# A trunk of four layers: TensorE's order in the third is written by hand, and its triangular blocks are inverted by doubling

## The chip, the cores and the metric

The kernel runs on one core of a Trainium2 chip. The metric is the device time of one execution in microseconds; for each kernel the median of several runs is given.

## What is computed

A trunk of four layers works on a sequence of 256 context and 1024 grid tokens with 1024 features: an RG-LRU layer, an mLSTM layer, an RWKV-7 layer (layer 2, the only one that the change touches) and an RG-LRU layer again. All in fp32. Cut to layer 2:

```python
def rwkv7_mixer(hc, hx, rows, ...):
    def run(h, shifted, states):
        xs = h[None] + (shifted - h)[None] * mu[:, None, None, :]          # six mixtures
        r, k, v, z = einsum('gbtd,gde->gbte', xs[:4], w_rkvz)
        w_pre = w0 + tanh(xs[4] @ w1) @ w2;  decay = exp(-exp(-softplus(-w_pre) - 0.5))
        a = sigmoid(a0 + (xs[5] @ a1) @ a2)
        kk = hd(k * k_k);  kk = kk / max(sqrt(sum(kk * kk)), 1e-12)
        ...
        yf, sf = rwkv7_scan(r, w[0], kk, a[0], k[0], v, states[0], False)   # forward
        yb, sb = rwkv7_scan(r, w[1], kk, a[1], k[1], v, states[1], True)    # backward
    ...
    return (finish(*parts_c) if with_ctx else None), finish(*parts_x)      # norm, bonus, gate, @ w_out

def rwkv7_scan(...):                                                       # per token
    s = s * w_t - (s @ kk_t) (kk_t * a_t)^T + v_t k_t^T;   y_t = s @ r_t
```

The kernel computes the scan in chunks of 64 tokens: inside a chunk the token recurrence becomes a unit triangular system of 64 x 64 for each head, which is inverted, and matmuls with the inverse carry the state from chunk to chunk.

## The kernel before

All of layer 2 is in `rwkv_scan`. The 1280 tokens are five blocks of 256, block 0 being the context. A batch `n` (0 to 39) is a pair of heads `e` and a place `i` in the order of the blocks: forward the blocks run 0, 1, 2, 3, 4, backward 0, 4, 3, 2, 1, and a batch holds both directions. Four pairs of heads follow each other at each `i`, so that the state of one pair, `st[e % 4]`, is needed again four batches later. Two waves of 20 batches cover the 8 pairs.

For each batch:
- `prep(n)` loads the projected rows, computes decay and gate, makes the operands `BK`, `AR`, `X`, multiplies them (line 1093) and cuts the products into the diagonal 32 x 32 blocks `DG`, the off-diagonal ones `OF`, and `RB`; it also transposes to `BT` (line 1111) and computes the bonus (line 1131).
- `inverse(n)` inverts the eight 64 x 64 triangles (2 directions, 4 chunks) of both heads: VectorE transposes `DG` to `LN` (line 1147, 1024 wide), inverts the 16 x 16 blocks by forward substitution in 14 pairs of small operations (lines 1164 and 1165), transposes back to `DF` (line 1167), and TensorE doubles twice: from 16 to 32 (lines 1177 and 1182, with the mask `DO` by GpSimd, `QQ` copied by ScalarE, `D32` added and `E32` transposed by VectorE) and from 32 to 64 (lines 1189 and 1195). The result is `DT`.
- `chain(n, step)` carries the state over one chunk in each direction: four groups of matmuls with a copy or an addition between them (lines 1236, 1240, 1246, then 1253 and 1255 for the output).
- `finish(n)` normalizes the output rows of a pair and writes them.

Beside the scan stand the projections: `group` (the mixtures made by `mixed`, eight operands of 128 features as a rounded part and a remainder, and then the products with the weights, three matmuls for each product) and `output` (the product with the output weights). `project` and the code for `v` (lines 924 to 926) issue them, `half` loads 512 columns of weights and splits them. `kk_norm` normalizes the keys. The list `fill` says which projections are issued in which iterations, and how many.

In an iteration of the main loop the code asks for four steps of `chain`, `finish(n - 2)`, `inverse(n + 1)`, `prep(n + 2)` and its share of the projections, in this order. This is no order on the engines: the kernel is built with a planner (`schedule_with_timeline_sim=True`) that lays out each engine's queue at compile time by its own estimate of when an instruction could start; `issue_after` only holds projections behind VectorE's work of three iterations ago. Each engine then takes its queue strictly in that order.

PSUM has eight banks: two for the projections (`pz`), two for `prep` and `finish` (`px`), three for the chain (`pc`), one for `inverse` and `kk_norm` (`pi`).

Of the kernel before, what the change touches and what calls it, by code (L numbers as in the profile page):

```python
# [28 lines left out]
class Net:  # L29
# [756 lines left out]
    def rwkv_scan(self, es, hd, zd, yd, xd):  # L786
# [107 lines left out]
        def project(w_ap, xs, n):  # L894
            ps = bank(pz, "pz")[:, 0:n]
            for k in range(len(xs)):
                if k % 4 == 0:
                    w = half(w_ap[:, k * 128:k * 128 + 512])
                self.mm3(ps, w, k % 4, xs[k], (0, n), k == 0, k == len(xs) - 1)
            return ps  # L900

# [3 lines left out]

        def group(blks, what, wave=0):
            n = 256 * len(blks)
            for g in what:
                xs = [mixed(g, k, blks) for k in range(8)]
                if g >= 4:  # L910
                    ps = project(self.a["r7_l1"][g - 4], xs, n)
                    t = tile_("po", [128, 512], bufs=3)
                    S.activation(out=t[:, 0:n], in_=ps, func=AF.Tanh if g == 4 else AF.Copy)
                    out_blocks(blks, lambda b: ld[b][:, g - 4, :], t)
                    yield
                elif g == 2:
                    for i, b in enumerate(blks):
                        for q in (wave,):
                            acc = [bank(pz, "pz") for _ in range(2)]
                            for k in range(8):  # L920
                                w = half(self.a["r7_wv"][q][:, k * 512:k * 512 + 512])
                                for c in range(2):
                                    tk = slice(i * 256 + c * 128, i * 256 + c * 128 + 128)
                                    mm(acc[c], xs[k][0][:, tk], w[0], start=k == 0, stop=False)
                                    mm(acc[c], xs[k][0][:, tk], w[1], start=False, stop=False)
                                    mm(acc[c], xs[k][1][:, tk], w[0], start=False, stop=k == 7)
                                if k == 3:
                                    yield
                            for c in range(2):
                                t = tile_("po", [128, 512], bufs=3)  # L930
                                S.copy(out=t, in_=acc[c])
                                for j in (0, 1):
                                    nc.sync.dma_start(out=vd[b][8 * q:8 * q + 8, :, 2 * c + j, :].rearrange("h s v -> s h v"),
                                                      in_=t[hr[j]].rearrange("p (h v) -> p h v", h=8))
                            yield
                else:
                    for e in range(4 * wave, 4 * wave + 4):
                        ps = project(self.a["r7_w"][g, e], xs, n)
                        t = tile_("po", [128, 512], bufs=3)
                        if g == 3:  # L940
                            S.activation(out=t[:, 0:n], in_=ps, func=AF.Tanh, scale=0.5)
                            self.stt(V, t[:, 0:n], t[:, 0:n], 1.0, ps, ALU.add, ALU.mult)
                            out_blocks(blks, lambda b: zd[e][:, b * 256:(b + 1) * 256], t)
                        else:
                            S.copy(out=t[:, 0:n], in_=ps)
                            out_blocks(blks, lambda b: krk[b][e, :, 1 - g, :], t)
                        if g == 1:
                            kk_norm(e, t, n, blks)
                        yield

        def output(blks, ks, src):

            n = 256 * len(blks)
            xs = []
            for k in ks:
# [8 lines left out]
                xs.append((hi, lo))  # L964
            s = 0 if blks[0] else 1
            for e in range(8):
                t = tile_("po", [128, 512], bufs=3)
                for i, b in enumerate(blks):
                    nc.sync.dma_start(out=t[:, i * 256:(i + 1) * 256], in_=src[e][:, b * 256:(b + 1) * 256])
                ps = project(self.a["r7_w_out"][e][:, ks[0] * 128:], xs, n)  # L970
                self.stt(V, t[:, 0:n], ps, gate[:, e, s:s + 1], t[:, 0:n], ALU.mult, ALU.add)
                out_blocks(blks, lambda b: xd[e][:, b * 256:(b + 1) * 256], t)
                yield

        def kk_norm(e, kt, n, blks):

            sq = tile_("kq", [128, 512], bufs=1)
            S.activation(out=sq[:, 0:n], in_=kt[:, 0:n], func=AF.Square, scale=kk_v[:, e:e + 1])
            nt = n // 128
            ps = bank(pi, "pi")  # L980
# [7 lines left out]
            ps = bank(pi, "pi")  # L988
# [27 lines left out]
        def prep(n):  # L1016
# [13 lines left out]
            DG = DGs[n % len(DGs)]  # L1030
            b["DG"], b["OF"] = DG, tile_("OF", [128, 8, 32])
            ts, ops = [], []
            for d in (0, 1):
# [43 lines left out]
                X = tile_("X%d" % d, [128, 4, 2, 128], bufs=3)  # L1077
                for hh in (0, 1):
                    r = hr[hh]
                    self.tt(G if hh else V, X[r, :, hh, :], AR[r], W[r].unsqueeze(2).to_broadcast([64, 4, 128]))  # L1080
                b[d] = dict(X=X, W=W)
                ts.append((t, rx))
                ops.append((BK, AR))
            for d in (0, 1):
                BK, AR = ops[d]
                X = b[d]["X"]
# [4 lines left out]
                for c in range(4):  # L1091
                    for hh, r in enumerate(hr):
                        mm(pss[hh][:, c * 128:(c + 1) * 128], BK[r, c, 64 - 64 * hh:192 - 64 * hh], AR[r, c, :], start=True, stop=True)  # L1093
                for hh in (0, 1):
# [12 lines left out]
            for d in (0, 1):  # L1107
                for c in range(4):
                    for hh in (0, 1):
                        o = d * 256 + c * 64  # L1110
                        nc.tensor.transpose(tp[hh][:, o:o + 64], ops[d][0][hr[hh], c, 64 - 64 * hh:192 - 64 * hh], self.ident[hr[hh], hr[hh]])
            for hh in (0, 1):
                S.copy(out=BT[:, :, :, hr[hh]], in_=tp[hh].rearrange("p (d c s) -> p d c s", d=2, c=4))
# [4 lines left out]
            else:  # L1118
                ps = bank(px, "px")
                for d in (0, 1) if i else (1,):  # L1120
# [8 lines left out]
                    for q in (0, 1):  # L1129
                        o = 4 * d * (i > 0) + 2 * q  # L1130
                        mm(ps[:, o:o + 2], tp[:, q * 128:(q + 1) * 128], rkb[:, e, :], start=True, stop=True)
                m = 8 if i else 4
# [5 lines left out]
        def inverse(n):  # L1138
# [5 lines left out]
            l8 = lambda name, tag=None: rp.tile([128, 8, 32], F32, tag=tag or name, name=name, bufs=1)  # L1144
# [4 lines left out]
            full = LN.rearrange("p t s -> p (t s)")  # L1149

            def ap(t0, tn, s0, sn, tb, sb):

                v = full[:, t0 * 32 + s0:t0 * 32 + s0 + 1]
                dims = [list(v.ap[0]), [16 * 33, 2], [0 if tb else 32, tn], [0 if sb else 1, sn]]
                return bass.AP(v.tensor, v.offset, dims)

            for j in range(1, 15):
                n1 = 15 - j
                tmp = tile_("ltmp", [128, 2, 56], bufs=1)
                c = ap(j + 1, n1, j, j, False, True)  # L1160
                x = ap(j, n1, 0, j, True, False)
                o = ap(j + 1, n1, 0, j, False, False)
                tv = tmp[:, :, 0:n1 * j].rearrange("p q (t s) -> p q t s", s=j)
# [4 lines left out]
            D16, E16 = l8("D16"), l8("E16", "E")  # L1168
            self.tt(V, D16, DF[:, 0:8, :], u8(m16))
            self.tt(V, D16, D16, u8(id32), ALU.add)  # L1170
            V.transpose(out=E16, in_=D16)
            p8 = lambda: pi.tile([128, 8, 64], F32, tag="pi", name="pi")
            ps = p8()
            g4 = [slice(32 * g, 32 * g + 32) for g in range(4)]
            for u in range(8):
                for g in g4:
                    mm(ps[g, u, 0:32], DO[g, u, :], E16[g, u, :], start=True, stop=True)
            QQ = l8("QQ", "Q8")
            S.copy(out=QQ, in_=ps[:, :, 0:32])
# [332 lines left out]
```

## Time and profile before

| | |
|---|---|
| median of 3 runs | 4717.35 us (4715.73 to 4727.37) |
| profiled execution | 4715.13 us |
| its span | 4713.0 us |
| TensorE busy | 4093.5 us (87%) |
| VectorE busy | 3313.9 us (70%) |
| GpSimd busy | 2271.5 us (48%) |
| ScalarE busy | 2110.1 us (45%) |
| granted clock of TensorE, mean | 0.855 |

Busy times are those of the profiled execution, the shares are of its span. A granted clock of 1.00 is 2.4 GHz, of 0.50 is 1.2 GHz; a value between is the mean over a stretch in which both were granted. Shares over the whole span mix four layers; the scan of layer 2 runs from about 2026 us to 4131 us of the span.

### The profile page before, as it was taken

Reading aid. Unit: us, or ns where it says so; the run is one execution under the profiler, and the core shown is the slowest. Engines: PE = TensorE matmul, PEld = TensorE weight load, DVE = VectorE, ACT = ScalarE, POOL = GpSimd, SP = SyncE. Lnnn points to the kernel's source line nnn. Section 1 sums busy time; section 2 is a strip of 40 time slices with the busy share of each in tenths; the row PEclk is TensorE's granted clock in tenths of the full one; section 3 lists DMA queues with packets and bytes.
Section 4 is the critical chain, followed back from the end, with each engine's and each line's share of the span. In section 5 each row is a group of like instructions: output and inputs, shape, how many; then the busy total and the mean of one; then the engine's idle time right before and its main releaser. Section 6 shows DMA issues by size and latency. Waiting matters only on the chain. (4 is left out here: it accounts for less than half of the span.)

```text
span 4713.0 us, 84318 instructions
## 1 busy us (share of the span) xinstructions
PE 4093.5 (87%) x32068; PEld 3313.0 (70%) x32068; DVE 3313.9 (70%) x6218; ACT 2110.1 (45%) x4476; POOL 2271.5 (48%) x1989
## 2 busy tenths in 40 slices
PE   6999888999999989668988888888898888779988
PEld 3687768988889868445667666666666676557767
DVE  4478656545545533687988888988889889658875
ACT  3576322222222210645656545445566434256661
POOL 2466533333333331366666545555456654356662
PEclk9999989999999999768788777667588787689989
DMA  5311422222222342434444333223244443321122
GB/s 202 116 51 51 141 90 77 90 88 92 88 88 88 116 136 71 157 119 131 139 134 142 121 102 109 88 91 106 85 139 129 148 154 114 100 99 52 47 95 97
DMA packets 317749, 504.50 MB, mean 107 GB/s; under 512 B 55168, under 2 KB 201600, under 8 KB 317216
## 3 DMA queue, kind: packets, MB, share of 16 engines
q1 hardware_dynamic: 317344, 499.12, 33.1%
q8 instruction: 252, 4.13, 0.4%
q14 instruction: 153, 1.25, 0.1%
HBM read 406.02 MB, written 92.96 MB: 106 GB/s over the span
## 5 line engine op out<-in xcount | busy, mean ns | idle before, releaser
L86 POOL TENSOR_TENSOR wlo<-wraw,whi 128x512 fp32r<-128x512 f32 (+3 forms) x437 | 713.8, 1635 | 922.5 <-DVE whi L101 453.3
L112 PE MATMUL pm<-hhi,wlo 128*128 128x512 f32 (+1 forms) x1648 | 611.9, 374 | 32.1 <-POOL wlo L86 32.1
L111 PE MATMUL pm<-hlo,whi 128*128 128x512 f32 (+1 forms) x1648 | 620.1, 377 | 9.9 <-DVE hlo L81 9.9
L110 PE MATMUL pm<-hhi,whi 128*128 128x512 f32 (+1 forms) x1648 | 617.7, 375 | 0.6 <-ACT hhi L288 0.6
L101 DVE CAST whi<-wraw 128x1024 fp32r<-128x1024 f32 (+4 forms) x189 | 170.0, 900 | 336.5 <-PE pm L111 171.1
L86 POOL TENSOR_TENSOR xl<-mx,xh 128x512 fp32r<-128x512 f32 (+1 forms) x240 | 288.6, 1205 | 221.1 <-ACT xh L881 181.7
L110 PE MATMUL pz<-xh,whi 128*128 128x512 f32 (+1 forms) x784 | 333.8, 428 | 51.2 <-ACT whi L890 22.0
L112 PEld LDWEIGHTS pm<-hhi,wlo 128*128 128x128 f32 x1648 | 316.0, 192 | 87.2 <-POOL wlo L86 37.8
L111 PEld LDWEIGHTS pm<-hlo,whi 128*128 128x128 f32 x1648 | 316.0, 192 | 65.8 <-DVE hlo L81 11.4
L110 PEld LDWEIGHTS pm<-hhi,whi 128*128 128x128 f32 x1648 | 316.8, 192 | 53.8 <-issue 1.7
L111 PE MATMUL pz<-xl,whi 128*128 128x512 f32 (+1 forms) x784 | 330.1, 422 | 22.1 <-POOL xl L86 18.2
L110 PE MATMUL pm<-yhi,whi 128*128 128x512 f32 (+1 forms) x816 | 303.9, 377 | 44.5 <-DVE x L81 16.2
L112 PE MATMUL pz<-xh,wlo 128*128 128x512 f32 (+1 forms) x784 | 329.5, 421 | 6.7 <-POOL wlo L86 4.9
L111 PE MATMUL pm<-ylo,whi 128*128 128x512 f32 (+1 forms) x816 | 304.7, 374 | 3.9 <-POOL ylo L86 3.3
L112 PE MATMUL pm<-yhi,wlo 128*128 128x512 f32 (+1 forms) x816 | 297.9, 372 | 1.6 <-POOL wlo L86 1.6
L81 DVE SCALAR_TENSOR_TENSOR x<-pm,mod,x 128x512 f32<-128x512 f32 (+1 forms) x208 | 136.6, 665 | 184.3 <-PE pm L112 168.2
L1093 PE MATMUL px<-AR,BK 64*128 64x128 f32 x1280 | 204.3, 362 | 67.1 <-ACT BK L1071 37.6
L110 PEld LDWEIGHTS pz<-xh,whi 128*128 128x128 f32 x784 | 175.5, 225 | 94.9 <-ACT xh L881 28.2
L1093 PEld LDWEIGHTS px<-AR,BK 64*128 64x128 f32 x1280 | 171.9, 253 | 93.4 <-ACT BK L1071 46.1
L890 ACT CAST whi<-wraw 128x512 fp32r<-128x512 f32 x276 | 169.7, 617 | 142.5 <-PE pz L111 47.6
L81 DVE SCALAR_TENSOR_TENSOR mx<-hp,vecs,mx 128x256 f32<-128x256 f32 (+3 forms) x280 | 198.4, 731 | 46.3 <-ACT mx L861 45.5
L1164 DVE TENSOR_TENSOR ltmp<-LN 128x28 f32<-128x28 f32 (+6 forms) x560 | 219.0, 391 | 12.1
(356 smaller groups left out, 11041.3 us busy)
## 6 DMA issues: line engine op xcount, KB each, us to landing
wraw<-in_r_w SPq DMA_DIRECT2D x144, 256.0 KB, 3.1
kin<-r7krk SPq DMA_DIRECT2D x72, 384.0 KB, 3.3
mw<-in_mod_w SPq DMA_DIRECT2D x48, 512.0 KB, 6.9
mw<-in_mod_w SPq DMA_DIRECT2D x96, 256.0 KB, 2.6
wraw<-in_lru_w_in SPq DMA_DIRECT2D x40, 512.0 KB, 3.6
hp<-r7h SPq DMA_DIRECT2D x160, 128.0 KB, 2.2
wraw<-in_r_wv SPq DMA_DIRECT2D x80, 256.0 KB, 3.1
UZ<-r7v SPq DMA_DIRECT2D x160, 128.0 KB, 2.9
```

Of the source, the lines that this page charges most:

```text
L81: i = eng.scalar_tensor_tensor(out=out, in0=in0, scalar=scalar, in1=in1, op0=op0, op1=op1, **k)
L86: eng.tensor_tensor(out=out, in0=a, in1=b, op=op)
L101: nc.vector.tensor_copy(out=hi, in_=raw)
L110: mm(out, w[0][:, c], x[0][:, a:a + b], start=first, stop=False)
L111: mm(out, w[0][:, c], x[1][:, a:a + b], start=False, stop=False)
L112: mm(out, w[1][:, c], x[0][:, a:a + b], start=False, stop=last)
L890: S.copy(out=hi, in_=raw)
L1093: mm(pss[hh][:, c * 128:(c + 1) * 128], BK[r, c, 64 - 64 * hh:192 - 64 * hh], AR[r, c, :], start=True, stop=True)
L1164: V.tensor_tensor(out=tv, in0=c, in1=x, op=ALU.mult)
```

## The change

`group` and `output` no longer issue their matmuls themselves. They yield passes (`rows` or `cols`), and `stream` issues one step of a pass at a time (three matmuls of up to 512 columns, or six for `v`), asks for weight halves two ahead, makes one operand of the next job behind each step of the pass before it, and puts the two later parts of `kk_norm` into the next pass, where they take a bank of `pz`. Each `yield` says what the step cost, one unit being a pass of 512 columns.

`prep`, `inverse`, `chain` and `finish` become generators with a `yield` between the pieces that wait for each other. In an iteration each piece has a time between 0 and 40 units; the pieces are issued in the order of these times, and between two of them `project` issues projections for `rate` units per unit of time. The amounts per iteration are 132 units (iterations 0 and 1), 84 (2 to 5), 46.5 (6 to 37) and 32 (38 to 40). At the end every TensorE instruction of the scan is tied behind the one before it, so that the planner can't change TensorE's order; the other engines' queues are still the planner's.

`inverse` no longer substitutes on VectorE. It starts from the blocks of size 1 (the identity) and doubles five times, sizes 1, 2, 4, 8 and 16, each time with a mask of `DG` (`lev`) by GpSimd; the first is an addition, the other four are the two groups of 32 matmuls that the last one was before, with ScalarE's copy between them and VectorE's addition and transpose behind. `DG` shrinks from 32 blocks to 8 and has two buffers.

The diff, cut (moved code of `group`, `output` and `prep` is left out where only its place changes):

```diff
+        def rows(job, w_ap, done):
+            n, ks = job.n, len(job.tiles)
+            hs = [w_ap[:, k * 128:k * 128 + 512] for k in range(0, ks, 4)]
+            def steps():
+                ps = bank(pz, "pz")[:, 0:n]
+                for k in range(ks):
+                    yield lambda w: self.mm3(ps, w, k % 4, job.xs[k], (0, n), k == 0, k == ks - 1)
+                done(ps)
+            return job, hs, 4, steps, 3 * n / 512
...
+        def stream(passes):
...
+            for pi_, (job, h, per, steps, cost) in enumerate(passes):
+                nxt = passes[pi_ + 1][0] if pi_ + 1 < len(passes) else job
+                while len(job.xs) < len(job.tiles):
+                    job.make()
+                if not ready:
+                    ahead()
+                for k, step in enumerate(steps()):
+                    if k % per == 0:
+                        if k:
+                            ready.pop(0)
+                        if len(ready) < 2:
+                            ahead()
+                    step(ready[0])
+                    if late and k in (2, 5):
+                        next(late[0], None)
+                        if k == 5:
+                            late.pop()
+                    if nxt is not job:
+                        nxt.make()
+                    yield cost
+                ready.pop(0)
+            drain(*late)
...
         def kk_norm(e, kt, n, blks):
             sq = tile_("kq", [128, 512], bufs=1)
             S.activation(out=sq[:, 0:n], in_=kt[:, 0:n], func=AF.Square, scale=kk_v[:, e:e + 1])
+            yield
             nt = n // 128
-            ps = bank(pi, "pi")
+            ps = bank(pz, "pz")
...
-            DO = l8("DO")
-            LN = tile_("LN", [128, 32, 32], bufs=1)
-            V.transpose(out=LN, in_=DG.rearrange("p u t -> p t u"))
-            self.tt(G, DO, DG[:, 0:8, :], u8(off16))
...
-            for j in range(1, 15):
...
-                V.tensor_tensor(out=tv, in0=c, in1=x, op=ALU.mult)
-                V.tensor_tensor(out=o, in0=tv, in1=o, op=ALU.add)
-            DF = tile_("DF", [128, 32, 32], bufs=1)
-            V.transpose(out=DF.rearrange("p u t -> p t u"), in_=LN)
...
+            O = l8("O")
+            self.tt(G, O, DG, u8(lev[0]))
+            D32, E32 = l8("D"), l8("E")
+            self.tt(V, D32, O, u8(id32), ALU.add)
             V.transpose(out=E32, in_=D32)
+            yield
+            for m in lev[1:]:
+                O = l8("O")
+                self.tt(G, O, DG, u8(m))
+                ps = p8()
+                for u in range(8):
+                    for g in g4:
+                        mm(ps[g, u, 0:32], O[g, u, :], E32[g, u, :], start=True, stop=True)
+                yield
+                QQ = l8("QQ", "Q8")
+                S.copy(out=QQ, in_=ps[:, :, 0:32])
+                for u in range(8):
+                    for g in g4:
+                        mm(ps[g, u, 32:64], QQ[g, u, :], D32[g, u, :], start=True, stop=True)
+                yield
+                D, E32 = l8("D"), l8("E")
+                V.tensor_tensor(out=D, in0=D32, in1=ps[:, :, 32:64], op=ALU.add)
+                V.transpose(out=E32, in_=D)
+                D32 = D
...
+        lev = [cst(f"lev{size}", [128, 32], 0.0) for size in (1, 2, 4, 8, 16)]
...
+            for m, size in zip(lev, (1, 2, 4, 8, 16)):
...
+                sel(v, [[-2 * size, nb], [0, size]], 0, 1)
+                sel(v, [[2 * size, nb], [0, size]], size - 1, -1)
...
+        fill = [(stream(group(G1, (4, 5) + krv)), 0, 2, 336), (stream(group(G2, (4, 5) + krv)), 2, 6, 336),
+                (stream(both(*(group(g, krv, 1) for g in (G0, G1, G2)), *(group(g, (3,), w) for g in (G0, G1, G2) for w in (0, 1)),
+                             output(G0, range(8), self.xsrc), output(G1, range(4), self.xsrc), output(G2, range(4), self.xsrc))), 6, 38, 1488),
+                (stream(output(G2, range(4, 8), xd)), 38, 41, 96)]
+        INV = (10, 12, 14, 16, 18, 20, 22, 24, 26, 28.5, 31, 33, 36)
...
+        for n in range(41):
+            dense, a, z, total = next(f for f in fill if f[1] <= n < f[2])
+            rate = (total - 72 * (a == 0)) / (z - a) / 40
...
+            for c, step, t in ((n - 1, 2, 0), (n - 1, 3, 16), (n, 0, 10), (n, 1, 26)):
+                if 0 <= c < 40:
+                    gens.append(at(chain(c, step), (t, t + 4, t + 8, t + 12, t + 14)))
+            if n < 39:
+                gens.append(at(preps[n + 1], (1, 5, 9, 11, 12)))
+                gens.append(at(inverse(n + 1), INV))
+            if n < 38:
+                preps[n + 2] = at(prep(n + 2), (13, 17, 19))
             if n > 1:
-                finish(n - 2)
+                gens.append(at(finish(n - 2), (3, 21, 23)))
+            t0 = 0
+            for t, _, g in sorted(events, key=lambda v: v[:2]):
+                if t > t0:
+                    project(rate * (t - t0))
+                    t0 = t
+                next(g, None)
+            project(rate * (40 - t0))
...
+        last = None
+        for i in nc.cur_bb.bb.instructions[mark:]:
+            if str(i.engine).split(".")[-1] == "PE":
+                if last is not None:
+                    self.tc.add_manual_dep(i, last.name, mybir.DependencyInfo(mybir.DependencyClass.NoSync, mybir.DependencyReason.DATA), reason="order")
+                last = i
```

## Rows read from the trace of the kernel before

**Rows 1.** Busy us of each engine in two stretches of the scan.

```profile
core 0: us, PE busy (x) PEld busy (x) DVE busy (x) ACT busy (x) POOL busy (x), PEclk, DMA share, GB/s
2026.00:2407.00 381.00, 305.61 (x2597) 217.86 (x2595) 319.50 (x592) 212.44 (x490) 242.42 (x225) 0.78 0.43 131
2407.00:4034.00 1627.00, 1379.56 (x16384) 1083.39 (x16383) 1418.06 (x3052) 844.70 (x2279) 897.73 (x963) 0.75 0.38 117
```

**Rows 2.** One line's instructions, 2407 to 4034: duration ns min/median/max, first, last start.

```profile
L1147 DVE STREAM_TRANSPOSE LN<-DG x34: 1932/1991/2124, 2407.0 to 4033.6; 128x1024 f32<-128x1024 f32 x34
```

**Rows 3.** Groups by line, 2020 to 4050: count | busy us, mean ns | idle before.

```profile
L1164 DVE TENSOR_TENSOR ltmp<-LN 128x28 f32<-128x28 f32 (+6 forms) x560 | 219.0, 391 | 12.1
L1165 DVE TENSOR_TENSOR LN<-ltmp,LN 128x28 f32<-128x28 f32 (+6 forms) x560 | 215.7, 385 | 12.7
...
L1147 DVE STREAM_TRANSPOSE LN<-DG 128x1024 f32<-128x1024 f32 x40 | 80.5, 2013 | 12.2 <-ACT DG L1099 11.5
...
L86 DVE TENSOR_TENSOR D<-DF,m 128x256 f32<-128x256 f32 x39 | 25.3, 650 | 0.5
...
L86 DVE TENSOR_TENSOR D<-D,id 128x256 f32<-128x256 f32 x39 | 21.7, 556 | 0.5
...
L1171 DVE STREAM_TRANSPOSE E<-D 128x256 f32<-128x256 f32 x39 | 16.9, 434 | 4.7 <-PE pi L1189 4.2
L1184 DVE TENSOR_TENSOR D<-D,pi 128x256 f32<-128x256 f32 x39 | 16.1, 414 | 10.7 <-PE pi L1182 10.3
```

**Rows 4.** The same view: one doubling level on the other engines.

```profile
L1177 PE MATMUL pi<-E,DO 32*32 32x32 f32 x2496 | 39.0, 209 | 17.9 <-DVE E L1171 13.1 <-DVE kq L81 4.8
...
L1182 PE MATMUL pi<-D,QQ 32*32 32x32 f32 x2496 | 36.8, 211 | 4.0 <-ACT QQ L1179 3.9
...
L86 POOL TENSOR_TENSOR DO<-DG,off 128x256 f32<-128x256 f32 x40 | 31.8, 795 | 31.6 <-ACT DG L1099 20.4 <-PE pi L1177 9.5 <-DVE ltmp L1164 1.6
...
L1179 ACT COPY QQ<-pi 128x256 f32<-128x256 f32 x39 | 14.5, 372 | 7.0 <-PE pi L1177 6.7
```

**Rows 5.** TensorE in order of time at granted clock 1.00: start us, us.

```profile
2626.97 0.50 PE L925 MATMUL pz<-wlo,xh 128*128 128x512 f32 x1
2627.31 0.39 PE L926 MATMUL pz<-whi,xl 128*128 128x512 f32 x1
2627.54 0.40 PE L925 MATMUL pz<-wlo,xh 128*128 128x512 f32 x1
...
2628.56 0.45 PE L1253 MATMUL pc<-UZ,X 128*64 128x64 f32 x8
...
2629.58 0.75 PE L1177 MATMUL pi<-E,DO 32*32 32x32 f32 x64
```

**Rows 6.** The same view at granted clock 0.50.

```profile
2605.74 1.08 PE L1182 MATMUL pi<-D,QQ 32*32 32x32 f32 x64 [3.91 <-ACT QQ L1179]
2606.75 0.80 PE L925 MATMUL pz<-wlo,xh 128*128 128x512 f32 x1
2607.34 0.63 PE L926 MATMUL pz<-whi,xl 128*128 128x512 f32 x1
2607.77 0.63 PE L925 MATMUL pz<-wlo,xh 128*128 128x512 f32 x1
...
3334.38 0.69 PE L1253 MATMUL pc<-UZ,X 128*64 128x64 f32 x8
```

**Rows 7.** Busy us of each engine in two stretches of one clock each (columns as rows 1).

```profile
2799.00:2829.00 30.00, 26.98 (x429) 21.41 (x419) 20.17 (x49) 15.74 (x42) 14.93 (x18) 1.00 0.39 120
...
3308.00:3427.00 119.00, 101.30 (x1252) 82.93 (x1251) 104.05 (x254) 62.94 (x180) 49.23 (x61) 0.50 0.28 81
```

**Rows 8.** Projections alone (bank pz): PE, PEld, DVE, ACT busy; clock, DMA, GB/s.

```profile
2799.00:2829.00 30.00, 10.18 (x41) 7.47 (x41) 0.00 (x0) 1.17 (x2) 1.00 0.39 120
...
3308.00:3427.00 119.00, 17.88 (x60) 13.54 (x59) 0.77 (x2) 1.93 (x4) 0.50 0.28 81
...
2407.00:4034.00 1627.00, 559.02 (x1939) 376.93 (x1938) 29.92 (x48) 34.33 (x65) 0.75 0.38 117
```

**Rows 9.** One tile's instructions: duration ns min/median/max, first and last start.

```profile
L812 POOL TENSOR_SCALAR_AFFINE_SELECT mk<-mk x8: 231/234/243, 1911.9 to 1914.3; 64x64 f32<-64x64 f32 x8
```

More of the change, by code (lines that the diff above doesn't have):

```diff
@@ L892, in half @@
             return hi, lo
[L894 to L900, printed above, removed]
         def out_blocks(blks, dst, t):
@@ new lines, in cols, with steps, mms @@
+        def cols(job, i, w_ap, done):
+            def steps():
+                acc = [bank(pz, "pz") for _ in range(2)]
+                for k in range(8):
+                    def mms(w):
+                        for c in range(2):
+                            tk = slice(i * 256 + c * 128, i * 256 + c * 128 + 128)
+                            mm(acc[c], job.xs[k][0][:, tk], w[0], start=k == 0, stop=False)
+                            mm(acc[c], job.xs[k][0][:, tk], w[1], start=False, stop=False)
+                            mm(acc[c], job.xs[k][1][:, tk], w[0], start=False, stop=k == 7)
+                    yield mms
+                for c in range(2):
+                    done(c, acc[c])
+            return job, [w_ap[:, k * 512:k * 512 + 512] for k in range(8)], 1, steps, 6
@@ new lines, in stream, with ahead @@
+        def stream(passes):
+            passes = list(passes)
+            hs = [ap for _, h, *_ in passes for ap in h]
+            ready = []
+            nh = 0
+            def ahead():
+                nonlocal nh
+                if nh < len(hs):
+                    ready.append(half(hs[nh]))
+                    nh += 1
+            for pi_, (job, h, per, steps, cost) in enumerate(passes):
[20 more added lines that the diff above has]
+            drain(*late)
@@ L916, in group @@
                 elif g == 2:
                     for i, b in enumerate(blks):
[L918 to L935, printed above, removed]
@@ L1167, in inverse @@
-            V.transpose(out=DF.rearrange("p u t -> p t u"), in_=LN)
[L1168 to L1171, printed above, removed]
+            l8 = lambda name, tag=None: rp.tile([128, 8, 32], F32, tag=tag or name, name=name, bufs=2 if name in "DO" else 1)
             p8 = lambda: pi.tile([128, 8, 64], F32, tag="pi", name="pi")
-            ps = p8()
             g4 = [slice(32 * g, 32 * g + 32) for g in range(4)]
-            for u in range(8):
-                for g in g4:
-                    mm(ps[g, u, 0:32], DO[g, u, :], E16[g, u, :], start=True, stop=True)
@@ L1178, in inverse @@
-            QQ = l8("QQ", "Q8")
-            S.copy(out=QQ, in_=ps[:, :, 0:32])
-            for u in range(8):
-                for g in g4:
-                    mm(ps[g, u, 32:64], QQ[g, u, :], D16[g, u, :], start=True, stop=True)
-            D32, E32 = l8("D32"), l8("E32", "E")
-            V.tensor_tensor(out=D32, in0=D16, in1=ps[:, :, 32:64], op=ALU.add)
-            V.transpose(out=E32, in_=D32)
+            O = l8("O")
+            self.tt(G, O, DG, u8(lev[0]))
+            D32, E32 = l8("D"), l8("E")
@@ L1314, in rwkv_scan @@
             nc.sync.dma_start(out=h0[k // 4][:, k % 4, :], in_=hd[k][:, 0:256])
-        for _ in group((0,), (4, 5, 1, 0, 2)):
-            pass
+        drain(stream(group((0,), (4, 5, 1, 0, 2))))
         early = False
@@ L1346, in rwkv_scan @@
         sgs = [cst(f"sg{d}", [128, 4, 65]) for d in (0, 1)]
-        DGs = [cst(f"DG{i}", [128, 32, 32]) for i in range(1)]
         DTs = [cst(f"DT{i}", [128, 8, 64]) for i in range(2)]
@@ new lines, in rwkv_scan, with project @@
+        INV = (10, 12, 14, 16, 18, 20, 22, 24, 26, 28.5, 31, 33, 36)
+        order_after = []
+        mark = len(nc.cur_bb.bb.instructions)
+        dense, debt = fill[0][0], 0.0
+        def project(amount):
+            nonlocal debt
+            debt += amount
+            while debt > 0:
+                with self.tc.issue_after(order_after[-3]) if len(order_after) >= 3 else ExitStack():
+                    c = next(dense, None)
+                if c is None:
+                    break
+                debt -= c
```

182 lines of the change are left out of this document (93 added, 89 removed).

## The prediction, made before the result was known

> **What bounds the kernel now.** I read the windows first, because the change touches layer 2 alone. The scan of layer 2 falls into a first stretch of 381 us and a steady stretch of 1627 us; the rest of the kernel is left as it is [rows 1]. In the steady stretch the reader is to see two engines near their limit: VectorE is busy for 1418.06 us (87%) and TensorE for 1379.56 us (85%), and TensorE's granted clock is only 0.75. ScalarE (844.70) and GpSimd (897.73) have room. To get from a stretch to one batch I count the batches by an instruction that each has once, the large transpose of line 1147: 34 of them start between 2407.0 and 4033.6, which makes 33 intervals of 49.3 us; 6 of the 40 lie in the first stretch [rows 2, 3]. Per batch that is 43.0 us of VectorE, 41.8 us of TensorE, 27.2 us of GpSimd, 25.6 us of ScalarE.
>
> Then I grouped by line, to see what of VectorE's 43 us is the inversion that goes, and last I read TensorE's order at both clock levels, since the second engine is the one that gets the work.
>
> **VectorE loses its role.** What the inversion of 16-wide blocks costs it: 560 multiplications and 560 additions (219.0 and 215.7 us), two large transposes of 80.5 us each (the second has the same size), a mask and an addition of the identity (25.3 and 21.7), two small transposes of 16.9 and one addition of 16.1 [rows 3]. That is 692.6 us, 17.3 per batch. In its place come, per batch, one addition of the identity (0.556 us), five small transposes (5 x 0.434) and four additions from PSUM (4 x 0.414): 4.4 us. Net minus 12.9: VectorE falls from 43.0 to 30.1 us per batch. These are the same forms of instruction, so I trust this term most.
>
> **TensorE gets more.** A doubling level is two halves of 32 small matmuls (64 records each in the trace). The one level of today takes 39.0 + 36.8 us in 39 batches, 1.94 us per batch [rows 4]. Four levels in place of one add 3 x 1.94 = 5.8 us. The step from 32 to 64 stays.
>
> The written order also cuts the projections into more pieces. The stream moves in steps of three passes of 512 columns. At the full level a pass starts 0.23 us after the one before it, but 0.34 after a pass that follows a small piece [rows 5]; at the low level 0.43 and 0.59 [rows 6]. So an entry costs 0.11 to 0.16 us. There are 46.5 units per batch, hence at most about 16 entries, 2.2 us at 0.14; if as many entries are there today, 0. I take 1.0. TensorE goes from 41.8 to 48.6 us per batch at today's mixture of clocks, and becomes the bound: the other three stand at 30.1 (VectorE), 27.2 + 4 x 0.795 = 30.4 (GpSimd, four more masks) and 25.6 + 3 x 0.372 = 26.7 us (ScalarE, three more copies) [rows 4].
>
> **The clock decides what 48.6 us are worth.** Prices at the levels of 2.4 and 1.2 GHz: a pass 0.23 and 0.43 us (ratio 1.87), eight records of the scan's matmuls 0.45 and 0.69 (1.53), 64 small records 0.75 and 1.08 (1.44) [rows 5, 6]. Projections are 559.02 of TensorE's 1379.56 us [rows 8], so a mean ratio of 1.65. If h is the share of time at 2.4 GHz, the work takes 1/(h + (1-h)/1.65) of its time at full clock: 1.245 at today's h of 0.5 (granted 0.75), 1.086 at h = 0.8 (0.90), 1 at h = 1.
>
> Which clock will it be? Compare two stretches of today. From 2799 to 2829 the clock stays at 1.00: TensorE is busy 26.98 of 30 us and projections are 10.18 of these, a third. From 3308 to 3427 it stays at 0.50 for 119 us: busy 101.30 us, 85% against 90%, but projections are only 17.88 us, 15% [rows 7, 8]. [...] Today the projections come in lumps, with bare scan between. Afterwards they are spread: 559.02/33 = 16.9 us per batch, 14.8 at a clock of 0.90, which is a third of an interval of 44.6 us. That sits by the good stretch. I take a granted clock of 0.90, and not 1.00, since the share is only about as high as in the one example, and a stretch that has fallen to 0.50 needs something dense to rise.
>
> **The sum.** TensorE busy for 95% of the interval (85% today, with VectorE in its way; between 90 and 98%). Steady: 48.6 x 1.086/1.245 = 42.4, over 0.95 is 44.6 us per batch against 49.3, minus 4.7, times 33: -155 us. First stretch: TensorE 305.61 us at a clock of 0.78 (h = 0.56, factor 1.21) [rows 1], plus 6 x 6.8 = 346.4; at 0.88 (factor 1.104) 316, over 0.95 is 333 against 381: -48. Sum -203. The profiled execution took 4715.1 us (span 4713.0), 2.2 below the median of the runs, so 4512, or 4514 beside the median: I say 4515.
>
> **What I cost at nothing.** The mixing of a group's operands is now made behind the steps of the pass before it: the same instructions, covered as long as GpSimd (30.4 us) is under the interval. The norm of the keys is cut in three and takes a bank of the projections' two; 20 of these, and if ScalarE's copy out of that bank is late, up to 0.7 us each, 14 us. No DMA is added; weight halves are asked for two ahead on the same queue, and a late one now stops TensorE, scan included. The masks of the levels are built by 40 selections in place of 8, 0.234 us each [rows 9], at most 7.5 us of GpSimd, ahead of the first batch, beside the projections of block 0.
>
> **The rivals.**
> *The clock doesn't rise* (slower). For: TensorE gets 6.8 us more per batch and two thirds of its time stay small matmuls, as in the stretch at 0.50. At 0.75 the interval is 48.6/0.95 = 51.2, +1.9 x 33 = +63, and the first stretch 346.4/0.95 = 365, -16: together +47, 4764 us. It decides from the point where TensorE's 48.6 us no longer fit 0.95 x 49.3 = 46.8: a granted clock below 0.79 in the steady stretch. Chance 0.10.
>
> *The written hops are too long* (slower). The inversion's 13 pieces are put at two units of 40, so an interval can't be shorter than 20 mean hops. A hop is a half (0.75 to 1.08 us) and then ScalarE's copy of 0.372, or VectorE's 0.414 and 0.434: 1.1 to 1.9 us without any queue, 1.5 in the mean. The engines behind are 60 to 70% busy with pieces of 0.3 to 1.3 us, so 0.5 us of queue is likely and 1.1 not excluded. At 2.6 us the interval is 52, +2.7 x 33 = +89, 4806 us; from 2.46 us per hop on there is no gain. TensorE takes its instructions in order, so each late hop stops the projections too. Chance 0.07.
>
> *The clock stays at full* (much faster). Even spreading may do away with all the stretches at 0.50. Then 48.6/1.245 = 39.0, over 0.95 is 41.1, -8.2 x 33 = -271; first stretch 346.4/1.21 = 286, over 0.95 is 301, -80; together -351, 4366 us. VectorE and GpSimd would be 73% busy, which allows it. Against it: the stretch at 0.50 idled little more than the one at 1.00. Chance 0.22. The Trainium skill (TensorE: Matmul & The Clock Gate, section HAM oscillation) says that long idle gaps between groups of matmuls are what throttles the array again and again; by that rule an order without such gaps keeps the full clock, which is this rival. The 119 us at 0.50 with TensorE 85% busy speak for more than gaps.
>
> *No difference* (within 0.3%, about what a measurement of this kernel can tell from none): the gain in clock just pays for the added matmuls, a clock of 0.79. Chance 0.05.
>
> **How the numbers follow.** The forecast has 0.56. Its own range: clock 0.85 to 0.95 and busy share 0.92 to 0.98, 4430 to 4610. Faster 0.56 + 0.22 = 0.78, same 0.05, slower 0.10 + 0.07 = 0.17. The range of 8 in 10 reaches to the lower rival's best third, which I leave out, and upward to just short of the clock that doesn't rise: 4330 to 4745.
>
> **What would show it.** VectorE's busy time in the scan falls by some 500 us, with no 1024-wide transposes; this is near certain. TensorE should be over 90% busy with a granted clock near 0.90 in each slice of the scan, with no stretch of 50 us at 0.50, and an interval of 44 to 45 us. Were the clock at 0.8 or lower with TensorE full, the first rival holds; were TensorE idle for over 15% with waits on the copies, additions and transposes of the inversion, the second. I would be most wrong if projections spread this thinly hold the clock less well than lumps do.

## The result, and the profile after

The changed kernel takes 5124.85 us (median of 4 runs, 5121.4 to 5132.78), 1.0869 times the kernel before [1.0839 to 1.0898]: 408 us slower where 203 us less were forecast. The profiled execution has a span of 5120.9 us, and everything outside the scan is as it was (2608 us in both kernels), so I compare the scan, from 2026 us to 582 us before the end in every kernel. It is 2513 us long, against 2105 before (the two stretches of [rows 1] and the tail), and 408 us is all of the difference.

The windows of the changed kernel over the scan, columns as in [rows 1]:

```profile
2026.00:4539.00 2513.00, 1862.61 (x35144) 1415.42 (x35143) 1347.77 (x2756) 1126.75 (x2944) 1248.76 (x1376) 0.77 0.33 101
```

TensorE is busy for 1862.61 us where it was 1754.6, and idle for 650 where it was 350: 108 us of the loss is work, 300 is waiting. VectorE fell from 1789.2 to 1347.77 us, 54% of the stretch, and yet nothing went faster. One batch by the transpose of line 1215, which each has once: (4432.8 - 2002.6)/39 = 62.3 us. Before, the transpose of line 1147 starts 40 times from 2026.1 to 4033.6 us, 51.5 us apart in the mean (49.3 in the steady stretch [rows 2]).

```profile
L1215 DVE STREAM_TRANSPOSE E<-D x40: 426/445/448, 2002.6 to 4432.8; 128x256 f32<-128x256 f32 x40
```

The groups by line of the changed kernel, for the work that the inversion has now (count | busy us, mean ns | idle before):

```profile
L1223 PE MATMUL pi<-E,O 32*32 32x32 f32 x10240 | 149.9, 218 | 287.4 <-DVE E L1233 285.0 <-DVE rn L1043 1.3 <-issue 0.7
L86 POOL TENSOR_TENSOR O<-DG,lev 128x256 f32<-128x256 f32 x197 | 146.5, 752 | 180.4 <-PE pi L1223 97.7 <-ACT DG L1160 67.6 <-DVE D L86 8.3
L1229 PE MATMUL pi<-D,QQ 32*32 32x32 f32 x10240 | 145.7, 213 | 27.8 <-ACT QQ L1226 20.6 <-issue 6.5
...
L1233 DVE STREAM_TRANSPOSE E<-D 128x256 f32<-128x256 f32 x160 | 70.2, 439 | 2.8
...
L1232 DVE TENSOR_TENSOR D<-D,pi 128x256 f32<-128x256 f32 x160 | 66.8, 417 | 143.9 <-PE pi L1229 140.7 <-ACT U L1291 1.7
...
L1226 ACT COPY QQ<-pi 128x256 f32<-128x256 f32 x160 | 59.3, 370 | 243.8 <-PE pi L1223 243.3
...
L86 DVE TENSOR_TENSOR D<-O,id 128x256 f32<-128x256 f32 x39 | 21.8, 558 | 0.5 <-POOL O L86 0.3
...
L1215 DVE STREAM_TRANSPOSE E<-D 128x256 f32<-128x256 f32 x39 | 17.3, 443 | 1.0
```

VectorE's inversion is 176 us in place of 692.6 [rows 3], as worked out. What the reader is to see stands at the end of the first line: TensorE is idle for 285 us because `E`, a transpose of 0.44 us on an engine that is busy half the time, isn't there. The longest waits of TensorE in this kernel (us in total, times, longest):

```profile
PE pi L1223 <- DVE E L1233: 285.0, 96, 8.2
PE px L1193 <- POOL tp L86: 64.9, 16, 6.0
PE px L1172 <- DVE X L1163: 53.8, 47, 2.7
PE pi L1238 <- DVE E L1233: 43.9, 18, 8.8
PE pc L1308 <- DVE UZ L81: 42.1, 19, 7.2
```

One such wait in order of time, TensorE and VectorE (start us, us; other engines and some lines left out):

```profile
3001.87 1.08 PE L1229 MATMUL pi<-D,QQ 32*32 32x32 f32 x64
...
3002.60 0.70 DVE L1086 CAST w<-w2r 64x256 fp32r<-64x256 f32 x1
...
3003.34 0.29 DVE L1109 TENSOR_SCALAR sg<-sg 128x256 f32<-128x256 f32 x1
...
3003.55 1.16 DVE L81 SCALAR_TENSOR_TENSOR UZ<-UZ,W,pc 64x64 f32<-64x64 f32 x4
...
3004.74 0.41 DVE L1126 TENSOR_SCALAR t<-ta,hka,oka 128x256 f32<-128x256 f32 x1
3005.07 0.69 DVE L1118 TENSOR_TENSOR_SCAN Q<-scm,sg 128x260 f32<-128x260 f32 x1
...
3005.67 0.88 DVE L81 SCALAR_TENSOR_TENSOR ta<-ta,kin 128x256 f32<-128x256 f32 x1
...
3006.59 0.42 DVE L1232 TENSOR_TENSOR D<-D,pi 128x256 f32<-128x256 f32 x1
3006.93 0.48 DVE L81 SCALAR_TENSOR_TENSOR AR<-kin,vecs,EN 128x256 f32<-128x256 f32 x1
...
3007.66 0.42 DVE L1130 TENSOR_TENSOR BK<-t,EP 128x256 f32<-128x256 f32 x1
...
3008.33 0.44 DVE L1233 STREAM_TRANSPOSE E<-D 128x256 f32<-128x256 f32 x1
...
3008.91 1.08 PE L1223 MATMUL pi<-E,O 32*32 32x32 f32 x64 [5.34 <-DVE E L1233]
```

The second half of a level ends at 3002.95. The addition `D` and the transpose `E` are 0.86 us of work, but work of the chain (`UZ`) and the preparation of the next batch stand before and between them on VectorE's queue, and `E` is done 5.8 us later. TensorE, in its written order, has nothing else that it may start: 5.34 us idle.

### The profile page after: what moved, and what is told of

Read it like the earlier page. It is cut to its first block, busy times and chain, and to the rows that moved or that the text cites. A ratio compares the mean times of both kernels' runs of the same rounds, so it can differ in the third digit from the quotient of the medians.

```text
span 5120.9 us, 114529 instructions
## 1 busy us (share of the span) xinstructions
PE 4197.6 (82%) x47428; PEld 3373.3 (66%) x47428; DVE 2883.2 (56%) x5216; ACT 2159.0 (42%) x4596; POOL 2356.8 (46%) x2188
## 5 line engine op out<-in xcount | busy, mean ns | idle before, releaser
L110 PE MATMUL pz<-xh,whi 128*128 128x512 f32 (+1 forms) x784 | 398.9, 509 | 22.0 <-DMA hp<-r7h 17.0
L1223 PE MATMUL pi<-E,O 32*32 32x32 f32 x10240 | 149.9, 218 | 287.4 <-DVE E L1233 285.0
L81 DVE SCALAR_TENSOR_TENSOR mx<-hp,vecs,mx 128x256 f32<-128x256 f32 (+3 forms) x280 | 212.0, 781 | 226.2 <-ACT mx L861 221.7
L1223 PEld LDWEIGHTS pi<-E,O 32*32 32x32 f32 x10240 | 132.7, 130 | 306.5 <-issue 271.6
L86 POOL TENSOR_TENSOR O<-DG,lev 128x256 f32<-128x256 f32 x200 | 149.2, 754 | 183.3 <-PE pi L1223 97.7
```

Source lines behind the costliest of these rows:

```text
L81: i = eng.scalar_tensor_tensor(out=out, in0=in0, scalar=scalar, in1=in1, op0=op0, op1=op1, **k)
L86: eng.tensor_tensor(out=out, in0=a, in1=b, op=op)
L110: mm(out, w[0][:, c], x[0][:, a:a + b], start=first, stop=False)
L1223: mm(ps[g, u, 0:32], O[g, u, :], E32[g, u, :], start=True, stop=True)
```

## Experiments

All kernels over the scan, from windows as above. The ratio is to the kernel before, measured again beside each, with its 95% interval; idle is TensorE's idle time, the clock its granted clock, the column VectorE its busy time, all in us but the ratio and the clock.

| kernel | ratio | scan us | TensorE busy | idle | clock | VectorE |
|---|---|---|---|---|---|---|
| before | 1 | 2105 | 1755 | 350 | 0.75 | 1789 |
| changed | 1.0869 [1.0839, 1.0898] | 2513 | 1863 | 650 | 0.77 | 1348 |
| e1 doubling alone | 1.0443 [1.0425, 1.0460] | 2315 | 1968 | 347 | 0.74 | 1389 |
| e2 no ties | 1.0144 [1.0128, 1.0159] | 2173 | 1867 | 306 | 0.79 | 1369 |
| e3 ties, substitution | 1.0694 [1.0678, 1.0710] | 2440 | 1736 | 704 | 0.73 | 1721 |
| e4 VectorE tied too | 1.1123 [1.1105, 1.1140] | 2636 | 1845 | 791 | 0.77 | 1307 |
| e6 no ties, substitution | 1.0020 [1.0007, 1.0034] | 2110 | 1758 | 352 | 0.75 | 1776 |
| e7 only the scan tied | 1.0834 [1.0811, 1.0858] | 2500 | 1867 | 633 | 0.72 | 1367 |
| e8 wide hops | 1.0633 [1.0612, 1.0654] | 2392 | 1823 | 569 | 0.79 | 1382 |
| e10 inversion untied | 1.0285 [1.0264, 1.0306] | 2237 | 1825 | 412 | 0.80 | 1387 |
| e11 hybrid, no ties | 0.9756 [0.9737, 0.9775] | 2007 | 1729 | 278 | 0.81 | 1608 |
| e12 before with the hybrid | 0.9991 [0.9976, 1.0006] | 2103 | 1798 | 305 | 0.77 | 1635 |
| e13 preparation cut | 1.0761 [1.0715, 1.0806] | 2466 | 1850 | 616 | 0.78 | 1357 |
| e14 the same, VectorE tied | 1.0879 [1.0833, 1.0925] | 2514 | 1848 | 666 | 0.78 | 1272 |

My theory after the result was the second rival of the prediction: TensorE in its written order waits at each level for VectorE. The rivals were that the doubling costs the time by itself, and that the cutting of the program does.

**One part of the change at a time.** e1 puts the new `inverse` (without its yields, with the masks and the smaller `DG`) into the kernel before.

> The kernel before with the inversion by doubling and nothing else: every queue, TensorE's too, is laid out by the planner. Theory of the hops (TensorE, held to a written order, stands before each doubling level until VectorE's addition and transpose have come through its queue): with the order free, other matmuls go ahead, so the 329 us of idle TensorE before lines 1223 and 1238 shrink to under 100, and the time lies near or under that of before, 4550 to 4800 us. Rival, the doubling itself (5.8 us more of TensorE per batch at a clock of 0.75): 40 x 5.8 = 232 us on top of 4717, 4900 to 5000 us, whatever the order.

e2 takes the ties out of the changed kernel:

```diff
-        last = None
-        for i in nc.cur_bb.bb.instructions[mark:]:
-            if str(i.engine).split(".")[-1] == "PE":
...
-                last = i
```

> The changed kernel without the ties at its end: the program is traced in the written order, but the planner may place TensorE's instructions as it does the others. Theory of the hops: the planner moves projections and scan pieces in front of the levels that wait, 4550 to 4850 us. Rival, that the way the program is cut (projections in single steps, the norm of the keys inside a pass, a bank of the projections for it) costs the time: 5000 to 5150 us, as with the ties.

e3 keeps the ties and has the old `inverse`, cut at its waits:

```diff
-        INV = (10, 12, 14, 16, 18, 20, 22, 24, 26, 28.5, 31, 33, 36)
+        INV = (12, 26, 28, 30, 32, 34, 36)
```

> The changed kernel with TensorE's order written and tied as it is, but the inversion by substitution on VectorE as before, its seven pieces at 12, 26, 28, 30, 32, 34 and 36 units. Theory of the hops: six hops in place of twelve behind VectorE, but the substitution's chain of 28 small operations has 14 units; 4700 to 4900 us, above before because a fixed order waits for VectorE, which stays 87% busy. Rival, that a fixed order alone costs nothing and only the doubling's hops do: 4500 to 4700 us. If the written order is the whole loss: 5050 us or more.

e6 is e3 without the ties.

> The changed kernel with neither the ties nor the doubling: its program cut into pieces and a steady stream of projections, the planner's order, substitution on VectorE. If the three parts add up as measured so far (doubling plus 210 us of busy TensorE, pieces and stream minus 140, ties plus 330), 4560 to 4640 us, below the kernel before, with a clock near 0.79 in the scan. Rival, VectorE as the bound: with 17.3 us of substitution per batch back it is 85 to 90% busy again and holds the time at that of before, 4680 to 4740 us.

e1 took 4927.36 us: the rival's 4900 to 5000, not mine. The doubling costs 213 us of TensorE's time (1968 against 1755), with as much idle time as before (347 against 350). It isn't all the same idle time: before the matmuls into `pi`, the bank of the inversion and the norm, it rose from 59 to 105 us, and before all others it fell from 291 to 242. e2 took 4787.0, as the theory of the hops has it. e3 took 5047.44, and the lines that were to set the theory apart from a bad order in general gave the latter, 3 us short of its 5050: 54 us more of TensorE's idle time than in the changed kernel, and with six hops in place of twelve. e6 took 4721.64, VectorE's rival: no gain.

With e6 the program of pieces and stream has been run with and without ties, and with either inversion. In it, the ties cost 6.7% with substitution (1.0694 - 1.0020) and 7.3% with doubling (1.0869 - 1.0144), 320 to 340 us of 4717 either way. Doubling costs 4.4% in the old program and 1.2% in the new. Pieces and stream alone change 0.2%. The ties were not put on the old program.

**Which part of the order.** In e7 the projections are left to the planner and only the scan's own TensorE instructions are tied; in e10 projections and scan are tied, and only the inversion is left out of the chain of ties:

```diff
-        for i in nc.cur_bb.bb.instructions[mark:]:
-            if str(i.engine).split(".")[-1] == "PE":
+        for at_, i in enumerate(nc.cur_bb.bb.instructions):
+            if at_ >= mark and at_ not in free and str(i.engine).split(".")[-1] == "PE":
```

(`free` holds what `inverse` issued in the loop; in e7 the same with what `project` issued.)

> The changed kernel with only the scan's own TensorE instructions tied in the traced order; the projections and the norm of the keys are left to the planner. If the harm of the ties is that projections stand fixed behind a piece that waits, so that nothing fills its wait, the time comes to that without ties, 4780 to 4860 us, and the idle time before line 1223 to under 100 us. Rival, that the order of the scan's pieces among themselves is what stops TensorE (a late inversion piece holds back chain and preparation): 5000 to 5130 us, idle before line 1223 over 200 us.

> The changed kernel with TensorE's instructions tied in the traced order, all but the inversion's, which the planner may place. If the inversion's fixed place between chain, preparation and projections is what stops TensorE, the waits for E before lines 1223 and 1238 fall from 329 us to under 100 and the time to 4780 to 4880 us, that without ties. Rival, that any order by hand of the scan stops as much (the waits for X, tp and UZ make up for it): 4950 to 5100 us.

e7 took 5109.32 us, the rival's side, with a wait of 257.3 us before line 1223: it isn't that projections can't fill a wait. e10 took 4857.34, the first of its two ranges. Freeing the inversion alone gives back 5.8 of the 7.3% (1.0869 - 1.0285); this was tried with the doubling only. The waits of TensorE in e10:

```profile
PE pi L1223 <- DVE E L1233: 82.2, 43, 4.4
PE pc L1308 <- DVE UZ L81: 46.4, 25, 4.4
PE px L1153 <- DVE X L1163: 44.8, 47, 2.6
```

The wait for `E` before line 1223 fell from 285.0 to 82.2 us (before line 1238 from 43.9 to 11.8), and the idle time from 650 to 412.

**The hops.** e8 places the inversion's pieces three units apart; the last three, not two, fall in the next iteration (40, 43 and 46):

```diff
-        INV = (10, 12, 14, 16, 18, 20, 22, 24, 26, 28.5, 31, 33, 36)
+        INV = tuple(range(10, 47, 3))
...
-                gens.append(at(inverse(n + 1), INV))
+                invs[n + 1] = at(inverse(n + 1), [t for t in INV if t < 40])
+            if n in invs:
+                gens.append(at(invs[n], [t - 40 for t in INV if t >= 40]))
```

> The changed kernel with all its ties, the inversion's 13 pieces three units apart in place of two, the last two of them in the next iteration. Theory of the hops as written in the prediction (an interval can't be shorter than the number of units over the spacing, times the mean hop): 20 hops per interval become 13.3, the wait for E falls from 329 us to under 180 and the time to 4800 to 4950 us. Rival, that each wait is for a queue that the planner has ordered against its own estimate, which more distance in TensorE's order doesn't mend: 5050 to 5200 us, the idle time moving to other pieces.

It took 5008.96 us, between the two ranges. The wait for `E` is still 265 us (208.9 and 56.1), 64 less than in the changed kernel, and the idle time is 81 less. The rule in my prediction, that an interval is so many mean hops long, is too simple: at 62.3 us in 20 hops a hop was 3.1 us, and 13.3 of these would be 41 us, no bound at all; the interval of e8 is 59.2 us ((4311.2 - 2003.4)/39).

**VectorE's queue.** e4 ties VectorE's instructions as well, in the traced order (the order in which the program issues them). e13 cuts preparation's elementwise work, traced in two lumps, into four pieces for each direction and spreads them; e14 is both.

```diff
+                yield
                 EN, EP = tile_("EN", [128, 4, 65]), tile_("EP", [128, 4, 65])
...
+                yield
                 self.stt(V, ta, ta, 1.0, kkx, ALU.add, ALU.mult)
...
+                yield
                 AR = tile_("AR", [128, 4, 128])
...
-                preps[n + 2] = at(prep(n + 2), (13, 17, 19))
+                preps[n + 2] = at(prep(n + 2), (13, 17, 21, 25, 29, 30, 32, 34, 37))
```

> The changed kernel with VectorE's instructions of the scan tied in the traced order too, so that each level's addition and transpose stand directly behind each other where the written order asks for them. Theory of the hops, in the form that the planner's order of VectorE makes them long (2.1 us from the second half to the addition, 1.35 more from the addition to the transpose, in the mean): TensorE's idle time before line 1223 falls from 285 to under 120 us, the time to 4750 to 4900 us. Rival, that the hops are long by their own latency: the idle time stays above 220 us and the time at 5050 to 5200; VectorE, which now also waits for each half in order, may make it worse.

> The changed kernel with all its ties; the elementwise work of preparation, traced in two lumps of some 5 us of VectorE at 17 and 19 units, is cut into four pieces for each direction and spread from 17 to 37 units between the inversion's additions (at 16, 20, 24 and 28.5). If that lump on VectorE's queue is what stands before the level's addition and transpose (in the changed kernel 481 us of other VectorE work stands there, some 340 of it preparation's), the wait before lines 1223 and 1238 falls from 329 us to under 180 and the time to 4850 to 5000 us. Rival, that the planner puts the work wherever its estimate says, however the program is cut: 5080 to 5160 us.

> The same with VectorE's instructions tied in the traced order too, in which the inversion's additions now stand between short pieces. If the lump is the cause, this helps more here than without VectorE's tie: 4850 to 5050 us against 5246 with the lumps. Rival, that VectorE in any fixed order stops for ScalarE and TensorE as much as it is stopped now: 5150 to 5300 us.

e4 took 5245.57 us, above both ranges: in the traced order too the lump comes ahead of the addition. Its expectation starts from hops of 2.1 and 1.35 us; over all 160 levels of the changed kernel the trace has 1.8 us from the end of a second half to the start of its addition, and 0.76 us from the addition's end to the start of the transpose. e13 took 5076.35, better than the changed kernel by 1.1%, 4 us below the rival's range; the wait for `E` fell to 203 us (172.8 and 30.0), but that for `UZ` rose from 42.1 to 93.1. e14 took 5131.32, between its two ranges. In e14 the lump is gone from `E`'s way, as its waits of TensorE show:

```profile
PE pc L1311 <- DVE UZ L81: 166.0, 70, 9.7
PE px L1156 <- DVE X L1166: 156.6, 49, 19.5
PE px L1196 <- POOL tp L86: 66.8, 16, 5.4
PE pi L1226 <- DVE E L1236: 37.4, 35, 6.8
```

The wait for `E` is 37.4 where e4 had 258.3, yet the idle time is 666 us. VectorE stands and waits for the second half, 319.2 us (301.9 in e4, 140.7 in the changed kernel), with the chain's and the preparation's work queued behind it:

```profile
DVE D L1235 <- PE pi L1232: 319.2, 132, 6.0
```

So with VectorE's order fixed the lump was what stood before `E`, but it is the smaller part of what the order costs. From e4 to e14 the wait for `E` lost 221 us and the idle time 125; without VectorE's tie, from the changed kernel to e13, the wait lost 126 and the idle time 34. The rest went to other waits.

**A version between.** The heavier load of e6 is VectorE's 1776 us, that of e2 TensorE's 1867. e11 substitutes within blocks of 8 (6 pairs of small operations, not 14) and doubles from there, without ties:

```diff
-                dims = [list(v.ap[0]), [16 * 33, 2], [0 if tb else 32, tn], [0 if sb else 1, sn]]
+                dims = [list(v.ap[0]), [8 * 33, 4], [0 if tb else 32, tn], [0 if sb else 1, sn]]
...
-            for j in range(1, 15):
-                n1 = 15 - j
+            for j in range(1, 7):
+                n1 = 7 - j
```

> No ties; pieces and stream as in the changed kernel; substitution on VectorE only within blocks of 8 (6 pairs of small operations in place of 14), then three doublings (8, 16 to 32, and the one to 64). VectorE loses 6 to 7 us per batch against substitution up to 16, TensorE gains 1.94. If neither engine alone but the larger of two loads sets the interval (43 us of VectorE in one, 48 of TensorE in the other), the time lies below both 4722 and 4787, 4600 to 4690 us. Rival, that the idle 15% come with the dependences whatever the loads are, so that TensorE's work sets the time: 4722 plus 30 to 80 us.

e12 puts the same `inverse` into the kernel before.

> The kernel before with the inversion of the hybrid alone (substitution within blocks of 8, then doublings), without the pieces and the steady stream. If the balance of VectorE and TensorE is what the hybrid wins by, 4600 to 4680 us, near the 4608 with the stream. Rival, that it needs the stream, which gave 140 us beside the full doubling and nothing beside substitution: 4700 to 4800 us.

e11 took 4608.07 us beside 4726.52 for the kernel before, 2.4% less, in the first of its ranges and faster than both kernels. Its windows over the scan:

```profile
2026.00:4033.00 2007.00, 1729.15 (x24909) 1332.42 (x24910) 1607.95 (x3173) 1090.39 (x2865) 1194.01 (x1255) 0.81 0.42 127
```

Both engines are below these loads, and the clock is the highest of all. e12 took 4713.83, no difference: the rival. Balance alone isn't enough; pieces and stream, which do nothing beside substitution, are worth 2.4% beside the hybrid and 3.0% beside the doubling. Why the two win only together was not tried further.

## Why the prediction was wrong

*VectorE's term was right.* 12.9 us less per batch were worked out; the inversion's rows fell by 692.6 - 176.1 = 516.5 us, 12.9 in 40 batches. VectorE as a whole lost 441, since other operations took longer (the mixing, for one, 779 ns against 733).

*The work added to TensorE was about right.* For the three more levels 232 us were taken (5.8 x 40); the two lines now take 295.6 us, 220 more than the one level of before, and e1 shows 213 more of busy time. For the entries into projections 1.0 us per batch was taken, between 0 and 2.2: line 110, which stands first in each step, went from 301.2 to 365.2 us with the same matmuls, some 700, 1.6 per batch. The terms put at nothing stayed near it: before all matmuls into the projections' banks, the norm's included, TensorE idles for 22 us in the changed kernel.

*The step that failed is "TensorE busy for 95% of the interval".* It was 74%, under the bound of 90 that I gave it. The forecast's sum has 30 us more of TensorE's work and 233 less of its idle time; the scan got 108 more of work and 300 more of idle time. So 533 of the 611 us between forecast and result are idle time. I took the 15% of idle time as VectorE's doing and let them go with VectorE's load, without a row on what TensorE waited for. The kernel before has these as its longest waits of TensorE in the scan:

```profile
PE pc L1236 <- DVE UZ L81: 50.4, 33, 4.5
PE px L1093 <- ACT BK L1071: 37.6, 17, 6.4
PE px L1093 <- DVE X L1102: 19.1, 18, 3.6
PE px L1111 <- DVE X L1102: 18.1, 11, 5.0
PE pi L1189 <- DVE E L1185: 16.7, 6, 7.4
```

The first four are for operands of the chain and the preparation; 59 of the 350 us in all stand before matmuls into the bank `pi` of the inversion and the norm. Even in the planner's order the sum of the idle time doesn't go: with VectorE down from 1789 to 1389 us, e1 has 347 us of it, and the scan is 210 us longer, near the 213 of the added matmuls. That is shown. It isn't shown that none of the 350 us was VectorE's: in e1 the waits before other matmuls shrank by 49 us and the doubling's own waits put 46 back, and in e12, with 154 us less of VectorE, 45 us of idle time went, for 43 us more of TensorE's work.

And a written order adds some 350 us of idle time of its own, whichever inversion it holds: 352 to 704 with substitution (e6, e3), 306 to 650 with doubling (e2, changed). I named the cost of an order that can't give way as a rival, with its place (behind the copies, additions and transposes of the inversion) and a chance of 0.07, and priced it at 4806. Its sign came: TensorE is idle for 26%, and 329 of the 650 us are waits for `E`. Its price by the number of hops was not right, since e3 idles longer with half the hops, and its chance was far too low: I had reckoned half a microsecond of queue per hop, from busy shares, where the trace has a mean of 1.8 us from the end of a second half to the start of its addition, and 0.76 more from its end to the start of the transpose.

*The clock was the second term that failed*: 0.90 forecast, 0.77 measured, and no run shows more than 0.81 (e11). I had taken it from the share of projections in two stretches of the kernel before, a third at 1.00 and 15% at 0.50. The changed kernel has that share, 872.88 of 2513 us (35%), and not the clock. It has a stretch at 0.50 with TensorE busy for 34.20 of 43 us and projections for 15.07, 35% of the stretch (all instructions, then bank `pz` alone; columns as in [rows 1], in the second line without GpSimd):

```profile
2794.00:2837.00 43.00, 34.20 (x652) 26.54 (x652) 17.37 (x43) 10.82 (x30) 13.79 (x17) 0.50 0.20 60
2794.00:2837.00 43.00, 15.07 (x36) 9.43 (x36) 0.87 (x2) 0.58 (x1) 0.50 0.20 60
```

Pieces and stream together raised the clock beside the doubling (0.74 in e1, 0.79 in e2) and beside the hybrid (0.77 in e12, 0.81 in e11), but not beside substitution (0.75 before and in e6). The forecast leaned on TensorE being full as well, and it was not, so what the clock would have been with a full TensorE stays open.

*What of the order costs it* is settled to this point: with the doubling, the inversion's fixed place takes 5.8 of 7.3% (e10), the projections' place next to nothing (e7: 1.0834 against 1.0869). Widening its steps gives back 2.4% (e8). Clearing VectorE's queue before it gives back 1.1% (e13), and nothing once VectorE is tied as well (e14), since most of the wait moves on. That a strict order of one engine can't be met by queues that the planner lays out by its own estimate, and that this holds for any order by hand, is argued, not shown; an order by hand that costs nothing may exist, and none was found.

## What to carry to other kernels

Idle time beside a busy engine isn't that engine's until a run without its load shows it: before counting on it, read what the idle engine waits for, take the load away and see whether the idle time goes. Fixing one engine's order makes every late operand stop everything behind it, and what one then sees in the waits is only the first of a row of such operands; leave the longest dependent chain free to slide first, which here gave back most of the cost. Where work can be split between two engines that are both near their limit, try the split between the two ends as well; here it paid only together with the steady stream.

## What the runs showed of the hardware that I had not expected

The written order made the scan's own matmuls cheaper. The same 1248 matmuls of the products in preparation (line 1093 before, 1153 after) took 200.1 us of TensorE's busy time before and 121.0 after; the 1280 of the chain's first group 144.5 and 83.5. In the traced order matmuls for the upper and the lower 64 rows alternate (rows of the operands in the products, of the result in the chain), and a group mostly stays together; the planner often splits it. Without the ties it is 176.1 (1232 matmuls in the window) and 123.5 in e2. That the alternation lets them overlap is a guess that was not tried. The two lines save 140 us, which is most of why TensorE's busy time rose by 108 us only, in spite of 220 from the levels and 64 from the entries. A version that keeps these groups together without tying the rest wasn't tried either.
